# Matmul with a rotary epilogue: block pairs loaded in half rows, one tile on each half of the partitions, with mirrored weights

## The chip, the cores and the metric

The kernel runs on one core of one Trainium2 chip. The metric is the device time of one launch in microseconds (us). The engines named below are TensorE (PE, with its weight loads shown apart as PEld), VectorE (DVE), ScalarE (ACT), GpSimd (POOL) and SyncE (SP, which only issues transfers and waits). SBUF is the memory on the chip with 128 partitions, PSUM the memory that TensorE writes to.

## The reference

A batch of 16 sequences of 512 rows and 768 columns is multiplied by a 768 x 768 weight matrix; each of the 12 heads of 64 columns is then rotated with given cosines and sines. All is float32; the kernel multiplies in float16.

```python
y = np.matmul(x, weight).reshape(16, 512, 12, 64)
y1, y2 = y[..., :32], y[..., 32:]
out1 = y1 * cos[..., :32] - y2 * sin[..., :32]
out2 = y2 * cos[..., 32:] + y1 * sin[..., 32:]
```

## The kernel before

**Tiles and groups.** The 8192 rows are cut into 64 tiles of 128 rows (i = 0 to 63). Four tiles make a group g = i // 4, two tiles a pair (g, h). A group's output of 4 x 768 columns fills six PSUM banks (`py`); pair h = 0 owns banks 0 to 2, pair h = 1 banks 3 to 5. The contraction over 768 is cut into six chunks (t, e) of 128.

**Two ways to bring the contraction onto the partitions.** TensorE needs x with the contraction index on the partitions.
- A plain tile is loaded whole by one transfer from SP (`load`, L201: 128 partitions x 3072 bytes into `xs`), cast to float16 by ACT (`cast`, L236, into `xc`), transposed on TensorE (`turn`, L244, or `turn_rows`, L256, which does it with 12 small matmuls on the two row halves of the array), and copied back from PSUM by ACT (into `xt`).
- A block pair (`BLOCKS`, L137: the second pair of groups 5 to 14, ten pairs) skips TensorE's transposes. It is loaded in four quarters (`load_quarter`, L209): quarter q puts columns 192 q to 192 q + 191 of both tiles on partitions 32 q to 32 q + 31, in runs of 768 bytes. Pairs of odd groups are loaded by SP as float32 into `xb` and cast by ACT (`cast_pair`, L274, into `xd`); pairs of even groups are loaded by POOL with the cast inside the transfer (into `xh`). Then one 32 x 32 block transpose on VectorE (`turn_pair`, L282) makes `xp`, in which the contraction lies on all 128 partitions for both tiles.

**Weights.** `load_w` (L225) loads each chunk's 128 rows with one transfer from SP into `w_raw`, VectorE casts it (`cast_w`) into `w_sb`. Loads at the start are issued by SP in the order of L459: tiles 0, 1, w0, tile 2, w1, w2, tile 3, w3, w4, w5, then the tables of cosines and sines, then tile 4 and on.

**The order of the work.** Group 0 is written out by hand (L528 to L635): each weight chunk is used by the tiles as it comes (`mm0`). From tile 4 to tile 59 the array is split in two row halves of 64 rows that work side by side on different banks: `walk` (L341) lists the matmuls of a pair for row half r, `one` (L355) issues one, and `both` (L372) takes always the half that is behind in columns (half 1 starts 1024 columns later, `LAG`). Each half contributes its 64 rows of every chunk, so every bank is written by both halves; the half that closes a bank waits until the other has closed its part (`after`). When banks are complete `rope` (L393) is issued: a multiply on VectorE (L411, PSUM times cos and sin into `tq` or the space of `w_raw`), then an add on POOL (L428) into `ov`, which is stored by ACT or SP.

**Queues.** Each engine takes its instructions in the order of issue. SP issues x loads in the order of the list `fetch` (L471 to L482), held back by the buffers: ten `xs`, three `xb`. `casts`, `turns` and `bturns` place ACT's and VectorE's work 6, 4 and 4 tiles ahead of the matmuls; POOL's quarters are issued 20 tiles ahead (`pool_loads`). Stores of most groups are delayed by a group or so (L603).

Of the kernel before, what the change touches and what calls it, by code (L numbers as in the profile page):

```python
# [10 lines left out]
FP32 = mybir.dt.float32  # L11
FP16 = mybir.dt.float16
# [93 lines left out]
def kernel(  # L106
# [11 lines left out]
    f = Flow(nc, tc)  # L118
    do = f.do
    P = nc.NUM_PARTITIONS  # L120

    B, S, H = x.shape
# [3 lines left out]
    R = 32  # L126
    NQ = P // R
    NT = H // (2 * P)
    SB = S // P
    QB = 4  # L130
    NG = B * SB // QB
    NTILE = QB * NG
    CHUNKS = [(t, e) for t in range(NT) for e in range(2)]
# [1 line left out]


    BLOCKS = {}  # L137
    for g in range(5, 15):
        BLOCKS[g, 1] = "pool" if g % 2 == 0 and g >= 4 else "sp"

    def sbuf(name, shape, dt):
        return nc.alloc_sbuf_tensor(name, shape, dt).ap()

    NX, NB, NBH, NC, NCP, NXT, NXP, NOV = 10, 3, 3, 5, 2, 8, 4, 4

    ident = sbuf("ident", [P, P], FP16)
    cold = sbuf("cold", [P, 512], FP16)
# [1 line left out]
    csn = sbuf("csn", [P, 2, SB, D], FP32)  # L149
    w_raw = sbuf("w_raw", [P, NT, 2, H], FP32)  # L150
    w_sb = sbuf("w_sb", [P, NT, 2, H], FP16)
    xs_b = [sbuf(f"xs{i}", [P, H], FP32) for i in range(NX)]
    xb_b = [sbuf(f"xb{i}", [P, 2 * H], FP32) for i in range(NB)]
    xh_b = [sbuf(f"xh{i}", [P, 2 * H], FP16) for i in range(NBH)]
    xc_b = [sbuf(f"xc{i}", [P, H], FP16) for i in range(NC)]
    xd_b = [sbuf(f"xd{i}", [P, 2 * H], FP16) for i in range(NCP)]
    xt_b = [sbuf(f"xt{i}", [P, NT, 2, P], FP16) for i in range(NXT)]
    xp_b = [sbuf(f"xp{i}", [P, 2 * H], FP16) for i in range(NXP)]
    tq_mem = sbuf("tq", [P, 6144], FP32)
    w_flat = w_raw.rearrange("p t e n -> p (t e n)")  # L160
    W_HOME = [f"wr{t}{h}" for t, h in CHUNKS]

    def products(at, n, lo, hi):

# [13 lines left out]
    def ring(name, n, state={}):  # L178
        k = state.get((id(f), name), 0)
        state[id(f), name] = k + 1  # L180
        return k % n

    def copy(e, o, i_):
        return lambda eng: (
            eng.copy(out=o, in_=i_) if e == "act" else eng.tensor_copy(out=o, in_=i_)  # L185
        )

    def where(i):
        g, s = divmod(i, QB)
        return QB * (g // SB) + s, g % SB  # L190

    def pair_of(i):
        return i // QB, (i % QB) // 2

    def is_block(i):
        return pair_of(i) in BLOCKS
# [10 lines left out]
            writes=[f"xs{k}"], dma=f"xs{k}")  # L207

    def load_quarter(gh, q):  # L209
        g, h = gh  # L210
        b, r = where(g * QB + 2 * h)
        e = BLOCKS[gh]
        src = x[b : b + 2].rearrange("b (j a r) (q k) -> r q a (b j) k", r=SB, a=R, q=NQ)
        if q == 0:
            xs[gh] = ring("xh", NBH) if e == "pool" else ring("xb", NB)
        k = xs[gh]
        name = f"xh{k}" if e == "pool" else f"xb{k}"
        buf = xh_b[k] if e == "pool" else xb_b[k]
        dst = buf.rearrange("p (j k) -> p j k", j=2 * NQ)
        do(e, lambda eng: eng.dma_start(out=dst[ts(q, R)], in_=src[r, q]),  # L220
           writes=[f"{name}q{q}"], dma=name)

    wv = weight.rearrange("(p t e) n -> t e p n", t=NT, e=2)

    def load_w(c, e="sp"):  # L225
        t, h = c
        do(e, lambda eng: eng.dma_start(out=w_raw[:, t, h], in_=wv[t, h]),  # L227
           writes=[f"wr{t}{h}"], dma=f"w{t}{h}")

    def cast_w(c, e):  # L230
        t, h = c
        do(e, copy(e, w_sb[:, t, h], w_raw[:, t, h]),
           reads=[f"wr{t}{h}"], writes=[f"w{t}{h}"])


    def cast(i, e):  # L236
        k = xs[i]
        c = ring("xc", NC)
        xc[i] = c
        do(e, copy(e, xc_b[c].rearrange("p (t m e) -> p t m e", t=NT, e=2),  # L240
                   xs_b[k].rearrange("p (m t e) -> p t m e", t=NT, e=2)),
           reads=[f"xs{k}"], writes=[f"xc{c}"])

    def turn(i, e):  # L244
# [29 lines left out]
    def cast_pair(gh, e="act"):  # L274
        k = xs[gh]
        c = ring("xd", NCP)
        xc[gh] = c
        do(e, copy(e, xd_b[c].rearrange("p (t j e) -> p t j e", t=NT, e=2),
                   xb_b[k].rearrange("p (j t e) -> p t j e", t=NT, e=2)),
           reads=[f"xb{k}q{q}" for q in range(NQ)], writes=[f"xd{c}"])  # L280

    def turn_pair(gh):  # L282
        g, h = gh
        z = ring("xp", NXP)
        dst = xp_b[z].bitcast(FP32)
        if BLOCKS[gh] == "pool":
            k = xs[gh]
            src = xh_b[k].bitcast(FP32).rearrange("p (j t) -> p t j", t=NT)
            rd = [f"xh{k}q{q}" for q in range(NQ)]
        else:  # L290
            c = xc[gh]
            src, rd = xd_b[c].bitcast(FP32), [f"xd{c}"]
        v = xp_b[z].rearrange("p (t m e) -> p t e m", t=NT, e=2)
        do("dve", lambda eng: eng.transpose(out=dst, in_=src), reads=rd, writes=[f"xp{z}"])  # L294
        for s in (0, 1):
            xT[g * QB + 2 * h + s] = (
                lambda t, e, s=s: v[:, t, e, ts(s, P)], f"xp{z}")

    def units(g):
        if g < LAST:
# [37 lines left out]

    def walk(pair, r):  # L341

        g, h = divmod(pair, 2)
        for bank in ((0, 1, 2) if r == 0 else (2, 0, 1)):
            opens = (r == 0) == (bank < 2)
            lo = h * 1536 + bank * 512
            parts = [(lo, lo + 512)] if bank != 1 else [(lo, lo + 256), (lo + 256, lo + 512)]
            for a, z in parts:
                i = g * QB + a // H
                for c in CHUNKS:  # L350
                    yield z - a, (g, i, a, z, r, c, opens,
                                  opens and (a, c) == (lo, CHUNKS[0]),
                                  c == CHUNKS[-1], z == lo + 512)

    def one(g, i, a, z, r, c, opens, start, ends, whole):  # L355
        s, rows, (t, h), bank = i % QB, ts(r, HP), c, a // 512
        get, key = xT[i]
        after = closed[g, bank] if not opens and c == CHUNKS[0] else 0
        do("pe", lambda eng: eng.matmul(  # L359
            py[:, a:z], get(t, h)[rows], w_sb[rows, t, h, a - s * H : z - s * H],  # L360
            start=start, stop=not opens and ends and whole, skip_group_check=True),
            reads=[key, f"w{t}{h}"], writes=[f"ps{bank}"], tick=ends, after=after)
        if ends and whole and opens:
            closed[g, bank] = f.count["pe"]
        if ends and whole and not opens:
            ready.setdefault(g, set()).add(bank)

    ready, roped = {}, set()
# [100 lines left out]


    fetch, quarters = [], []  # L471
    soon = [p for p in sorted(BLOCKS) if BLOCKS[p] == "sp"]
    for i in range(QB, NTILE):
        if soon and i >= max(2, soon[0][0] - 1) * QB:
            quarters += [(soon[0], q) for q in (0, 2, 1, 3)]
            soon.pop(0)
        if not is_block(i):
            fetch.append(i)
            if quarters:
                fetch.append(quarters.pop(0))  # L480
        elif quarters and quarters[0][0] == pair_of(i):
            fetch.append(quarters.pop(0))  # L482
# [4 lines left out]
    def pump():  # L487

        while fetched[0] < len(fetch):
            j = fetch[fetched[0]]  # L490
            if isinstance(j, int):
                if xs_sent[0] - xs_used[0] >= NX:
                    return
                load(j)
                xs_sent[0] += 1
            else:
                if j[1] == 0:
                    if xb_sent[0] - xb_used[0] >= NB:
                        return
                    xb_sent[0] += 1  # L500
                load_quarter(*j)
            fetched[0] += 1
# [56 lines left out]
    pump()  # L559

    rows_on = [False]
    state = {"cast": 4, "turn": 4, "bturn": 0, "pool": 0}
    pairs = sorted(BLOCKS)
    pool_pairs = [p for p in pairs if BLOCKS[p] == "pool"]

    def casts(upto, most=NTILE):
        while state["cast"] < min(upto, NTILE) and most > 0:
            most -= 1
            i = state["cast"]
            state["cast"] += 1  # L570
            if not is_block(i):
                castx(i, "act")
            elif i % 2 == 0 and BLOCKS[pair_of(i)] == "sp":
                cast_pair(pair_of(i))
                xb_used[0] += 1
            pump()
# [14 lines left out]
            turn_pair(gh)  # L591
            state["bturn"] += 1

    def pool_loads(upto):
        while state["pool"] < len(pool_pairs):
            gh = pool_pairs[state["pool"]]
            if gh[0] * QB + 2 * gh[1] >= upto:
                return
            for q in (0, 2, 1, 3):
                load_quarter(gh, q)  # L600
            state["pool"] += 1

    stores = {}  # L603
    for g in range(LAST):
        for h in (0, 2):
# [9 lines left out]
                q = q[:3] + ("sp",)  # L615
            stores.setdefault(i, []).append(q)

    C_AHEAD, T_AHEAD, B_AHEAD, P_AHEAD = 5, 3, 4, 20

    for i in (0, 1):  # L620
        mm0(i, CHUNKS[5])
# [15 lines left out]
    for i in range(QB, NTILE):  # L637
# [22 lines left out]
        bturns(i + B_AHEAD)  # L660
        turns(i + 1 + (T_AHEAD if i > QB else 2), 1)
        casts(i + 1 + (C_AHEAD if i > QB else 4), 1 + i % 2)
        pool_loads(i + P_AHEAD)
        for q in stores.get(i, ()):
            store(*q)
        if g == LAST:
# [47 lines left out]
```

## Time and profile before

| what | value |
|---|---|
| median of 3 runs | 152.18 us (151.9 to 154.3) |
| the profiled execution | 152.72 us, of which the span of its instructions is 150.9 us |
| PE busy | 140.2 us (93%) |
| DVE / POOL / ACT busy | 126.8 / 122.0 / 78.3 us |
| DMA moved | 51.27 MB, mean 340 GB/s |
| loads issued by SP / by POOL, stores by ACT | 27.92 MB with the SP stores / 1.97 MB as written (float16) / 21.10 MB |

The span runs from the first instruction to the last; some 1.8 us of the execution lie around it. Busy shares are means over stages with different limits, so a stage has to be read by itself: what ended the last wait there. Durations of transfers from issue to landing include the time that they stand in the queue.

### The profile page before, as it was taken

What the parts mean: (1) busy time and instruction counts of PE and PEld (TensorE: products, weight loads), DVE (VectorE), ACT (ScalarE), POOL (GpSimd) and SP (SyncE); (2) the same over time, 40 slices, a digit from 0 to 9 for tenths busy, and PEclk for the clock granted to TensorE, in tenths of its full rate; (3) what the DMA queues carried; (4) which work ended last, traced back from release to release, by engine and by line L of the source; (5) the groups of instructions that cost most, each with busy time, mean ns of one, the idle gap of its engine ahead of it and who ended that gap; (6) DMA issues with size and microseconds to landing.
All of it is one profiled execution on the core that took longest, in us unless ns stands there. A gap on an engine that the chain in (4) does not pass through costs nothing.

```text
span 150.9 us, 4381 instructions
## 1 busy us (share of the span) xinstructions
PE 140.2 (93%) x1938; PEld 101.2 (67%) x1938; DVE 126.8 (84%) x93; ACT 78.3 (52%) x92; POOL 122.0 (81%) x67
## 2 busy tenths in 40 slices
PE   6659999999999999999999999999999999999930
PEld 2325557778777777777777777777777777776620
DVE  0244997887888899899999998999989998999990
ACT  3444688977787842548243826283436826164000
POOL 1000387799989997999999999999995979999970
PEclk9999999999999999999999999999999999999995
DMA  4999999999999999999999999999999999976574
GB/s 125 340 382 403 402 399 398 243 402 326 306 365 340 290 351 358 322 383 344 339 350 384 376 324 356 363 387 329 351 364 404 417 394 401 385 278 240 221 297 151
DMA packets 27555, 51.27 MB, mean 340 GB/s; under 512 B 7184, under 2 KB 13072, under 8 KB 27536
## 3 DMA queue, kind: packets, MB, share of 16 engines
q1 hardware_dynamic: 14592, 27.92, 53.9%
q10 hardware_dynamic: 7504, 21.10, 35.6%
q0 software_dynamic: 5440, 1.97, 10.5%
q8 instruction: 15, 0.25, 0.6%
q14 instruction: 4, 0.03, 0.1%
HBM read 27.79 MB, written 25.17 MB: 351 GB/s over the span
## 4 chain that ended last, share of the span: by engine, by line
PE 86%; DMA 5%; DVE 4%; SPq 1%; issue 1%; ACT 1%; DVEq 0%
PE py L359 72%; PE py L334 8%; DMA w_raw<-in_weight_dram 5%; PE pt L266 4%; PE pt L251 1%; DVE tq L411 1%; DVE ov L428 1%; DVE xs L411 1%; SPq L205 1%; SPq L227 1%; ACT xt L185 1%; DVE w_sb L185 0%; SPq L709 0%; DVEq L57 0%; SPq L116 0%
## 5 line engine op out<-in xcount | busy, mean ns | idle before, releaser
L428 POOL TENSOR_TENSOR ov<-tq 128x1536 f32<-128x1536 f32 (+3 forms) x29 | 75.4, 2620 | 19.9 <-DVE tq L411 19.8
L359 PE MATMUL py<-w_sb,xt 64*128 64x256 f16 (+1 forms) x864 | 80.7, 323 | 0.0
L411 DVE TENSOR_TENSOR tq<-py,csn 128x1024 f32<-128x1024 f32 (+2 forms) x45 | 74.1, 1676 | 5.4 <-PE py L359 5.0
L359 PEld LDWEIGHTS py<-w_sb,xt 64*128 64x128 f16 x864 | 53.3, 94 | 17.6 <-DVE tq L411 0.4
L185 ACT COPY xt<-pt 128x768 f16<-128x768 f16 x42 | 33.5, 800 | 42.1 <-PE pt L266 38.0
L185 ACT CAST xc<-xs 128x768 f16<-128x768 f32 x44 | 39.2, 905 | 18.2 <-DMA xs<-in_x_dram 17.9
L359 PE MATMUL py<-w_sb,xp 64*128 64x256 f16 (+1 forms) x480 | 46.8, 323 | 0.0
L411 DVE TENSOR_TENSOR w_raw<-py,csn 128x1024 f32<-128x1024 f32 (+1 forms) x21 | 35.2, 1676 | 4.4 <-PE py L359 4.2
L428 POOL TENSOR_TENSOR ov<-w_raw 128x1536 f32<-128x1536 f32 (+1 forms) x12 | 35.0, 2921 | 3.7 <-DVE w_raw L411 3.4
L359 PEld LDWEIGHTS py<-w_sb,xp 64*128 64x128 f16 x480 | 30.4, 94 | 9.5
L334 PE MATMUL py<-w_sb,xt 128*128 128x256 f16 (+1 forms) x90 | 15.7, 323 | 1.9 <-DVE w_sb L185 1.6
L266 PEld LDWEIGHTS pt<-ident,xc 64*128 64x128 f16 x432 | 14.1, 95 | 1.8 <-ACT xt L185 0.6
L334 PEld LDWEIGHTS py<-w_sb,xt 128*128 128x128 f16 x90 | 8.1, 98 | 7.7 <-DVE w_sb L185 3.2
L266 PE MATMUL pt<-ident,xc 64*128 64x64 f16 x432 | 12.4, 190 | 0.3 <-ACT xt L185 0.3
L220 POOL DMA_DIRECT2D xh<-in_x_dram x20 | 11.6, 589 | 0.0
L185 ACT CAST xd<-xb 128x1536 f16<-128x1536 f32 x5 | 8.2, 1638 | 0.1
L185 DVE CAST w_sb<-w_raw 128x768 f16<-128x768 f32 x6 | 3.4, 560 | 4.4 <-DMA w_raw<-in_weight_dram 4.4
L294 DVE STREAM_TRANSPOSE xp<-xh 128x768 f32<-128x768 f32 x5 | 6.2, 1237 | 0.0
L510 PE MATMUL py<-cold 128*128 128x512 f16 x12 | 4.2, 512 | 1.4 <-DVE cold L453 1.4
L185 DVE COPY xt<-pt 128x768 f16<-128x768 f16 x2 | 1.1, 558 | 4.9 <-PE pt L251 4.9
L251 PE MATMUL pt<-ident,xc 128*128 128x128 f16 x48 | 4.0, 220 | 0.9 <-ACT xc L185 0.9
L251 PEld LDWEIGHTS pt<-ident,xc 128*128 128x128 f16 x48 | 2.9, 98 | 3.0 <-ACT xc L185 2.0
(17 smaller groups left out, 15.4 us busy)
## 6 DMA issues: line engine op xcount, KB each, us to landing
out_dram<-ov ACTq DMA_DIRECT2D x26, 768.0 KB, 9.1
xs<-in_x_dram SPq DMA_DIRECT2D x44, 384.0 KB, 16.8
xb<-in_x_dram SPq DMA_DIRECT2D x20, 192.0 KB, 16.1
out_dram<-ov SPq DMA_DIRECT2D x4, 768.0 KB, 3.9
w_raw<-in_weight_dram SPq DMA_DIRECT2D x6, 384.0 KB, 7.7
xh<-in_x_dram POOLq DMA_DIRECT2D x20, 96.0 KB, 13.2
out_dram<-ov SPq DMA_DIRECT2D x1, 384.0 KB, 2.3
out_dram<-ov ACTq DMA_DIRECT2D x1, 384.0 KB, 2.3
```

The source lines that it names most:

```text
L185: eng.copy(out=o, in_=i_) if e == "act" else eng.tensor_copy(out=o, in_=i_)
L205: do(e, lambda eng: eng.dma_start(out=xs_b[k], in_=x[b].rearrange("(p r) h -> r p h", r=SB)[r]), writes=[f"xs{k}"], dma=f"xs{k}")
L220: do(e, lambda eng: eng.dma_start(out=dst[ts(q, R)], in_=src[r, q]), writes=[f"{name}q{q}"], dma=name)
L227: do(e, lambda eng: eng.dma_start(out=w_raw[:, t, h], in_=wv[t, h]), writes=[f"wr{t}{h}"], dma=f"w{t}{h}")
L251: do("pe", lambda eng: eng.transpose(pt[:, t, h, :], src[:, t, h, :], ident), reads=[f"xc{c}", "ident"], writes=[f"pt{k}"], tick=(t, h) == ...
L266: do("pe", lambda eng: eng.transpose(pts[r][:, t, h, :], src[rows, t, h, :], ident[rows, rows]), reads=[f"xc{c}", "ident"], writes=[f"pt{r ...
L294: do("dve", lambda eng: eng.transpose(out=dst, in_=src), reads=rd, writes=[f"xp{z}"])
L334: do("pe", lambda eng: eng.matmul(ps, get(t, h), w_sb[:, t, h, a - s * H : z - s * H], start=start, stop=stop), reads=[key, f"w{t}{h}"], w ...
L359: do("pe", lambda eng: eng.matmul(py[:, a:z], get(t, h)[rows], w_sb[rows, t, h, a - s * H : z - s * H], start=start, stop=not opens and en ...
L411: do("dve", lambda eng: eng.tensor_tensor(out=tq.rearrange("p j (h d) -> p j h d", d=D), in0=ps.rearrange("p (h d) -> p h d", d=D) .unsque ...
L428: do(adder, lambda eng: eng.tensor_tensor(out=ov_b[o][:, ds(c0, w)].rearrange("p (h t d) -> p h t d", t=2, d=HD), in0=tq[:, 0].rearrange(" ...
L510: do("pe", lambda eng: eng.matmul(py[:, ts(b, 512)], cold[:, 0:P], cold, start=True, stop=warmed[0] < WARM - 6), reads=["cold"], writes=[f ...
```

## The change

Twelve pairs (the second pair of groups 3 to 14) are block pairs, and SP loads all of them as float32; POOL issues no transfer, and `xh`, its cast inside the transfer and `pool_loads` are gone. `xb` has four buffers. A quarter now holds half rows of one tile: quarters 0 and 1 put the two halves of the rows of the first tile on partitions 0 to 63, quarters 2 and 3 those of the second tile on partitions 64 to 127, in runs of 1536 bytes. After VectorE's transpose, a tile's whole contraction lies on its own 64 partitions in 12 chunks of 64, and row half r of the array does tile r alone. For that each half of the partitions needs all weight rows: `w_sb` holds one half, and `w_un` gets the other by two transfers inside SBUF (`mirror`), issued by SP at tile 14's place in `fetch`. The rows of the weights are numbered so that plain tiles use the same `w_sb`; each chunk of the weights is loaded by two transfers of 64 partitions instead of one of 128. In `walk` a block pair's bank 0 and bank 2 are written by one row half only, bank 1 by both. Quarters stand in `fetch` at their own pair's place.

```diff
-    for g in range(5, 15):
-        BLOCKS[g, 1] = "pool" if g % 2 == 0 and g >= 4 else "sp"
+    for g in range(3, 15):
+        BLOCKS[g, 1] = "sp"
-    NX, NB, NBH, NC, NCP, NXT, NXP, NOV = 10, 3, 3, 5, 2, 8, 4, 4
+    NX, NB, NC, NCP, NXT, NXP, NOV = 10, 4, 5, 2, 8, 4, 4
+    w_un = sbuf("w_un", [P, NT, 2, H], FP16)
...
-        src = x[b : b + 2].rearrange("b (j a r) (q k) -> r q a (b j) k", r=SB, a=R, q=NQ)
+        b, r = where(g * QB + 2 * h + q // 2)
+        src = x[b].rearrange("(j a r) (q k) -> r q a j k", r=SB, a=R, q=2)[r, q % 2]
...
-    wv = weight.rearrange("(p t e) n -> t e p n", t=NT, e=2)
+    wv = weight.rearrange("(m u t e) n -> t e u m n", u=2, t=NT, e=2)
...
-        do(e, lambda eng: eng.dma_start(out=w_raw[:, t, h], in_=wv[t, h]),
-           writes=[f"wr{t}{h}"], dma=f"w{t}{h}")
+        for u in range(2):
+            do(e, lambda eng: eng.dma_start(out=w_raw[ts(u, HP), t, h], in_=wv[t, h, u]),
+               writes=[f"wr{t}{h}{u}"], dma=f"w{t}{h}")
...
-        do(e, copy(e, xc_b[c].rearrange("p (t m e) -> p t m e", t=NT, e=2),
-                   xs_b[k].rearrange("p (m t e) -> p t m e", t=NT, e=2)),
+        do(e, copy(e, xc_b[c].rearrange("p (t u m e) -> p t u m e", t=NT, u=2, e=2),
+                   xs_b[k].rearrange("p (m u t e) -> p t u m e", t=NT, u=2, e=2)),
...
+    def mirror():
+        for u in range(2):
+            do("sp", lambda eng: eng.dma_start(
+                out=w_un[ts(1 - u, HP)].rearrange("p t e n -> p (t e n)"),
+                in_=w_sb[ts(u, HP)].rearrange("p t e n -> p (t e n)")),
+                reads=[f"w{t}{h}" for t, h in CHUNKS], writes=[f"v{u}"], dma=f"v{u}")
...
+        if gh in BLOCKS:
+            plan = ([("only", [(0, 512)]), ("close", [(512, 768)])] if r == 0 else
+                    [("open", [(768, 1024)]), ("only", [(1024, 1536)])])
...
+                    for t in range(2 * NT):
+                        own = (t < NT) == (r == 0)
+                        u, tt = t // NT, t % NT
+                        for c in range(2):
+                            w = (w_sb if own else w_un)[rows, tt, c, n0 : n0 + cols]
...
-        if soon and i >= max(2, soon[0][0] - 1) * QB:
+        if soon and i >= soon[0][0] * QB + 2 * soon[0][1] - 4:
...
+        if i == soon_mirror:
+            fetch.append("mirror")
```

## The prediction

> **What bounds the kernel now.** I read the page's first two parts and its chain, then the timelines of VectorE, PE and ACT over the start, then the table by windows.
>
> ```profile
> span 150.9 us, 4381 instructions
> PE 140.2 (93%) x1938; PEld 101.2 (67%) x1938; DVE 126.8 (84%) x93; ACT 78.3 (52%) x92; POOL 122.0 (81%) x67
> ...
> PE   6659999999999999999999999999999999999930
> ...
> PE 86%; DMA 5%; DVE 4%; SPq 1%; issue 1%; ACT 1%; DVEq 0%
> ```
>
> PE is dense from the fourth slice to the last two, and the chain of work lies on it for 86%. So only two kinds of edit show in the time: what changes PE's own work, and what delays it. The 5% that the chain spends on DMA is the wait for the weights at the start. VectorE's timeline shows when they land, since it casts each at once:
>
> ```profile
> 9.71 0.56 DVE L185 CAST w_sb<-w_raw 128x768 f16<-128x768 f32 x1 [1.38 <-DMA w_raw<-in_weight_dram]
> 10.65 0.56 DVE L185 CAST w_sb<-w_raw 128x768 f16<-128x768 f32 x1 [0.38 <-DMA w_raw<-in_weight_dram]
> 12.62 0.56 DVE L185 CAST w_sb<-w_raw 128x768 f16<-128x768 f32 x1 [1.40 <-DMA w_raw<-in_weight_dram]
> 13.59 0.56 DVE L185 CAST w_sb<-w_raw 128x768 f16<-128x768 f32 x1 [0.42 <-DMA w_raw<-in_weight_dram]
> 14.59 0.56 DVE L185 CAST w_sb<-w_raw 128x768 f16<-128x768 f32 x1 [0.43 <-DMA w_raw<-in_weight_dram]
> ```
>
> Neighbours in the queue land 0.97 us apart (10.65 and 9.71; 13.59 and 12.62): 0.393 MB in 0.97 us is 405 GB/s, and the queue is never empty, for the third weight is issued at 3.27 us and lands at 10.63. Behind the weights stand the tables and tile 4, which lands at 16.28; ACT casts it at once, and PE's chain takes it at once:
>
> ```profile
> 12.74 0.33 PE pt L251 x6
> 13.08 4.25 PE py L334 x26
> 17.33 0.43 PE pt L251 x6
> 17.76 0.65 PE py L334 x4
> 18.41 0.35 PE pt L251 x6
> 18.76 0.33 PE py L334 x2
> 19.09 2.17 PE py L359 x16
> ```
>
> (start, length, what). The transpose at 17.33 is tile 4's, whose cast ends at about 17.25; the one at 18.41 is tile 5's, landed at 17.25. Group 0's banks, too, come free for PE only after products that need the last weight. So PE has no slack here: whatever delays the sixth weight and tile 4 delays PE's dense run, and the end, one for one.
>
> How fast transfers go depends on their shape and their company:
>
> ```profile
> 14.00:20.00 6.00, 6.00 (x46) 3.09 (x45) 5.24 (x7) 3.62 (x5) 1.85 (x2) 1.00 1.04 402
> 27.00:30.00 3.00, 3.00 (x50) 2.15 (x47) 2.34 (x3) 2.64 (x4) 2.74 (x1) 1.00 1.05 232
> 30.00:34.00 4.00, 4.00 (x73) 3.04 (x71) 3.27 (x3) 2.95 (x5) 3.98 (x6) 1.00 1.03 397
> 100.68:108.83 8.15, 8.15 (x134) 6.19 (x126) 8.00 (x6) 3.67 (x5) 7.88 (x3) 1.00 1.14 343
> 35.00:43.50 8.50, 8.50 (x147) 6.54 (x145) 7.03 (x5) 6.40 (x8) 8.47 (x3) 1.00 1.15 318
> ```
>
> (window, length, busy time of PE, PEld, DVE, ACT, POOL, clock, DMA share, GB/s.) Loads over all 128 partitions alone: 402. The same queue with quarters of 32 partitions among the tiles and no stores yet: 232, with the engines as busy; a tile's packet of 3072 bytes then takes about 226 ns instead of 121 to 125. With stores beside them: 397.
>
> **The change part by part.** The sum is made against the profiled execution, 152.72 us (150.9 us of span, 1.8 around it), which is 0.54 above the median of 152.18.
>
> *PE's transposes.* Two plain pairs (groups 3 and 4) become block pairs: four turns of 0.18 us (the chain's steps of L266, 12 matmuls each) go, -0.72. The windows agree: a group without a block pair takes 8.50 us, with one 8.15; two groups, -0.70. The matmuls stay: 2 x 9216 columns per pair, 24 per row half before (6 chunks x 4 pieces) and after (12 chunks x 2 pieces), and the halves still use different banks. Waits of one half for the other fall from three a pair to one; the chain shows none that costs, so nothing is gained.
>
> *VectorE.* 12 block transposes of 0.97 us (the form from `xd`) in place of 5 of 0.97 and 5 of 1.24: +0.6. It is busy 8.00 of 8.15 us in a group with such a pair, so it still fits; were the new layout to cost 1.24 it would need 8.27 a group, as the groups with a POOL pair do now without holding PE. Taken 0, bound 1.4 (12 x 0.12).
>
> *ACT.* Seven more casts of 1.63, four casts of 0.905 and four copies of 0.80 fewer: +4.6 us, under 3.67 of 8.15 us busy per group. The casts read pairs of numbers 48 bytes apart instead of 24, which no row shows; both casts cost 0.95 ns per further element ((1638 - 905) / 768), so I take the same. 0.
>
> *POOL.* 20 issues of 0.589 us (11.6 us) go. It waits for products, not PE for it: 0.
>
> *Transfers in the middle.* The cast transfers of POOL go, 5120 packets of 49 ns, and 5120 of SP's at 47; 6144 packets of 1536 bytes come, between 65 ns (on the line from 36 at 768 bytes to 121 at 3072) and 113 (half the 226). Four plain tiles go (512 packets of 130). In engine time over 16 engines: -30.7 - 4.2 + (25 to 43) = -10 to +8 us, in stages with stores nearer the first, since quarters took 36 ns beside stores once POOL's were done. `mirror` adds 1.18 MB: 2.9 us of queue at 405 GB/s, 5.1 at 232. Cover: tile 16 lands 7.0 us before its cast, tile 17 5.7, tile 20 none but 2.2 us before its transpose; and two pairs (1.57 MB, 4 us) that were loaded ahead of tile 20 now stand behind it. The copies must also land before tile 14's matmuls at about 41 us; tile 13 lands at 26, then quarters (2 to 3.4 us) and copies (2.9 to 5.1): 37 at the latest. Taken 0, bounds 0 and +1.5 (tile 20: 2.2 + 4 - 5.1 - 2.9 at worst). SP's 28 more quarter issues cost 0.43 each, 12 us, on a queue that stands blocked by full rings for most of 27 to 108 us: 0.
>
> *The weights at the start.* Six transfers of 128 partitions become twelve of 64. Six more issues of 0.43 us do not show: SP is 7 us ahead. The transfers are the same packets of 3072 bytes, so they cannot be faster than 405 GB/s: lower end 0. No row has a 64-partition load; the nearest is the stretch of 27 to 30 us, part-partition loads among tiles with no stores, as at the start: 232 GB/s, 1.69 us a weight instead of 0.97, 6 x 0.72 = +4.3. If tiles 2 and 3 among them slow down as the tiles did there, 8 x 0.72 = +5.8, the upper end. I take +4.3, since nothing else in the trace is as near: no stores, one queue, parts of the partitions. It goes to the end in full (above).
>
> [...]
>
> Sum: -0.7 + 4.3 = +3.6; 152.72 + 3.6 = 156.3 for a profiled run, 155.8 against the median.
>
> **The rivals.**
> - *The halves overlap at the start* (the other side: not slower). The 16 engines do not stay in step: one tile's shares landed between 14.89 and 16.28 us. If an engine that is ahead works on the second half while its neighbour is on the first, both halves of the memory are written at once and a weight still takes 0.97 us. For it: the first quarters at 26 us still ran at 36 ns a packet, full speed. Against it: a microsecond later everything fell to half, and stayed so until stores came. Then 152.18 - 0.7 = 151.5. In between (a third of the loss, 1.4) 152.9. It decides at a delay of 0.7 us: below that the time is no longer than before.
> - *The middle runs dry.* Copies and quarters fall into a stretch without stores and ACT's casts wait, so PE's transposes do: the start's +4.3 and 1.5 to 3 more, 157.3 to 158.8. For it: tiles 33, 37, 41, 45, 49 and 53 are cast in the very moment they land, so the loads are the scarce thing there, and tile 53's transpose begins only 2.3 us after its cast. Against it: the engine time above falls beside stores, and quarters no longer run a group ahead of the tiles.
> - *Part of the delay is swallowed.* For it: PE has 0.9 us of idle time at 21.6, where it waits for ACT. Against it: ACT's work there follows the same loads. 155.8 - 0.9 = 154.9.
>
> **How the numbers follow.** A difference of about 2%, 3.0 us, is what a measurement of this kernel can tell from no change: 155.2 is the bound. The likeliest case, weights at about half rate: 50%, 154.9 to 157.5, a tenth of it under the bound. Halves that overlap: 25%, 151.3 to 152.6. In between, swallowed in part or half overlapped: 13%, 152.6 to 154.9. The middle runs dry as well: 12%, 157.3 to 158.8 and a little over; 0.10 of it above the bound, 0.01 after a fast start, and 0.01 I keep for a gain. Slower: 0.45 + 0.10 = 0.55. Within 2%: 0.05 + 0.25 + 0.13 + 0.01 = 0.44. Faster by over 2%: 0.01; PE alone would have to lose 3 us of work, and the change takes 0.7. The range leaves out a tenth or less at each end: 151.5 to 158.5.
>
> **What would show it.** Right: VectorE's casts of the weights 1.5 to 1.9 us apart where they were 0.97, the last at 18 to 20 us instead of 14.59; PE's first L359 at 22.5 to 24 instead of 19.09; GB/s of the second to fourth slice well under 340 to 400; a group of 8.15 us from group 3 on and no PE gap between. Wrong: weight casts still 0.97 us apart (the first rival), or waits of PE for ACT or for the copies between 35 and 60 us (the second); a transpose of 1.24 or a slower cast would show in the groups' rows.

## The result and the profile after

The changed kernel takes 163.52 us in the median of 4 runs (162.22 to 165.09); the kernel before took 152.7 beside it (4 runs). The ratio is 1.0699, 95% interval 1.0587 to 1.0810: slower by 10.8 us, where 3.6 were forecast. The profiled execution of after is its longest, 165.09 us with a span of 163.3. In this section and the next a ratio leaves disturbed runs out, so it is not always the quotient of the two medians, and the profiles of after, of the halves on two queues, of the middle partitions and of twelve pairs by SyncE are of such runs. The median of the kernel before, taken anew beside each set of runs, was 151.8 to 152.7 us, so a difference between runs of different sets is good to about 1 us.

The page of after, its parts on busy time, slices and the chain:

```profile
span 163.3 us, 4302 instructions
PE 145.5 (89%) x1890; PEld 110.9 (68%) x1890; DVE 128.3 (79%) x95; ACT 82.0 (50%) x91; POOL 110.9 (68%) x47
...
PE   6759899898986898999999989889999999999950
...
GB/s 153 287 257 239 324 404 249 269 237 321 402 363 218 306 408 258 371 409 358 387 359 360 386 381 365 332 400 323 412 364 408 334 417 387 414 394 328 265 313 169
...
DMA 32%; PE 29%; SPq 26%; ACT 4%; DVE 3%; issue 3%; DVEq 0%
```

PE's slices have holes from the fifth on, and the chain, which lay on PE for 86%, now lies on transfers and on SyncE's queue for 58%. The GB/s row moves between about 240 and 400, slice by slice. Two places explain the time. First the start, in VectorE's timeline of after (weight casts) and then PE's:

```profile
10.37 0.56 DVE L185 CAST w_sb<-w_raw 128x768 f16<-128x768 f32 x1 [2.12 <-DMA w_raw<-in_weight_dram]
12.00 0.56 DVE L185 CAST w_sb<-w_raw 128x768 f16<-128x768 f32 x1 [1.07 <-DMA w_raw<-in_weight_dram]
14.98 0.56 DVE L185 CAST w_sb<-w_raw 128x768 f16<-128x768 f32 x1 [2.42 <-DMA w_raw<-in_weight_dram]
16.62 0.56 DVE L185 CAST w_sb<-w_raw 128x768 f16<-128x768 f32 x1 [1.08 <-DMA w_raw<-in_weight_dram]
18.26 0.56 DVE L185 CAST w_sb<-w_raw 128x768 f16<-128x768 f32 x1 [1.07 <-DMA w_raw<-in_weight_dram]
```

```profile
22.58 2.39 PE L376 MATMUL py<-w_sb,xt 64*128 64x512 f16 x19
...
50.24 0.35 PE L264 MATMUL pt<-ident,xc 64*128 64x64 f16 x12 [1.82 <-ACT xt L185]
...
53.97 3.51 PE L376 MATMUL py<-w_sb,xt 64*128 64x512 f16 x40 [0.78 <-ACT xt L185]
```

Neighbouring weights land 1.63 us apart instead of 0.97, the last cast is at 18.26 instead of 14.59, and the dense run begins at 22.58 instead of 19.04: 3.54 us. The last two lines belong to the second place, the middle: PE waits for ACT's copies. ACT's waits in after, from the list of waits (total, times, longest), and the first of them in before, against which they stand:

```profile
ACT xc L185 <- DMA xs<-in_x_dram: 34.3, 18, 4.0
ACT xd L185 <- DMA xb<-in_x_dram: 15.9, 10, 2.4
```

```profile
ACT xc L185 <- DMA xs<-in_x_dram: 17.9, 9, 3.1
```

Before, nine tiles were waited for and no pair; after, 18 tiles and 10 of 12 pairs. ACT's timeline of after shows how such a wait reaches PE:

```profile
45.17 0.88 ACT L185 CAST xc<-xs 128x768 f16<-128x768 f32 x1 [3.98 <-DMA xs<-in_x_dram]
48.62 0.87 ACT L185 CAST xc<-xs 128x768 f16<-128x768 f32 x1 [2.57 <-DMA xs<-in_x_dram]
48.62 0.39 ACTq L465 DMA_DIRECT2D out_dram<-ov  x1
49.40 0.79 ACT L185 COPY xt<-pt 128x768 f16<-128x768 f16 x1
51.55 1.57 ACT L185 CAST xd<-xb 128x1536 f16<-128x1536 f32 x1 [1.37 <-DMA xb<-in_x_dram]
53.03 0.79 ACT L185 COPY xt<-pt 128x768 f16<-128x768 f16 x1
```

The cast at 48.62 waits 2.57 us for a tile; the copy behind it ends at 50.19, and PE's transpose starts at 50.24. The cast at 51.55 holds the copy at 53.03, and PE starts at 53.97. ACT's store, too, is issued only at 48.62, behind the cast: while ACT waits for loads no new store starts. What that does to the loads is in the windows of after (columns as before):

```profile
23.00:33.00 10.00, 9.21 (x154) 6.39 (x154) 7.66 (x5) 7.84 (x11) 8.12 (x4) 1.00 1.07 277
33.00:40.00 7.00, 6.33 (x103) 5.64 (x98) 6.08 (x4) 5.53 (x6) 4.73 (x2) 1.00 1.00 271
40.00:47.00 7.00, 6.92 (x102) 5.57 (x103) 5.53 (x6) 1.68 (x2) 4.55 (x2) 1.00 1.04 400
49.00:55.00 6.00, 3.98 (x53) 2.55 (x55) 3.29 (x4) 4.23 (x5) 3.77 (x2) 1.00 1.08 220
23.00:148.00 125.00, 118.30 (x1725) 95.97 (x1723) 108.74 (x69) 71.00 (x79) 98.16 (x32) 1.00 1.04 354
```

and of before over its own dense run:

```profile
23.00:33.00 10.00, 10.00 (x177) 7.68 (x173) 8.12 (x5) 8.12 (x12) 8.11 (x7) 1.00 1.05 340
23.00:140.00 117.00, 117.00 (x1758) 88.43 (x1753) 107.73 (x69) 65.69 (x78) 110.08 (x54) 1.00 1.06 351
```

The DMA share, last column but one, is above 1 in both: on the mean the engines that move data had a packet under way all the time before, too. (It is a sum of packet times over 16 engines, so at 1.06 and 1.04 some packets of one engine overlapped.) The copies were issued at 20.54 and 21.08 us and landed at 40.46 and 43.16; tile 16, which before landed at 30.86, lands at 45.15 and is cast in that moment (the first line of ACT's timeline); in the run without the copies, below, it lands at 36.05. From there on the loads only keep pace.

The account in the two profiled executions, by the start of the last run of products (138.62 before, 151.34 after, +12.7): 3.5 at the start, -0.7 for four turns saved, and 9.9 between, of which 8.0 lie in eleven stalls of PE of 0.1 to 2.0 us, between 31 and 132 us (counted from start to start of its matmuls, less the usual 0.2; a short wait at 26.05 is in before too, at 22.49). The other 1.9 was not traced. Nine of the eleven follow a copy of ACT. Two, at 31.41 and 40.08 (0.7 each), show no releaser, but the transfers offer one: packets of 16384 bytes on the queue that the profile calls "instruction" landed at 29.81 and 38.45, and PE goes on 1.60 and 1.63 us later. In the run with whole weights, below, such packets landed at 25.69 and 34.65, and PE goes on after a stall without releaser at 27.22 and 36.16, 1.53 and 1.51 us later. So these two look like PE waiting for its own instructions, brought through the same crowded transfers; no run tested it. The profiled run being 1.6 us above its median, the middle costs some 8 us in the median: 10.8 - 3.5 + 0.7.

### The profile page after: what moved, and what is told of

The parts are those of the page before. It is cut to its first block, busy times and chain, and to the rows that moved or that the text cites. A ratio compares the mean times of both kernels' runs of the same rounds, so it can differ in the third digit from the quotient of the medians.

```text
span 163.3 us, 4302 instructions
## 1 busy us (share of the span) xinstructions
PE 145.5 (89%) x1890; PEld 110.9 (68%) x1890; DVE 128.3 (79%) x95; ACT 82.0 (50%) x91; POOL 110.9 (68%) x47
## 4 chain that ended last, share of the span: by engine, by line
DMA 32%; PE 29%; SPq 26%; ACT 4%; DVE 3%; issue 3%; DVEq 0%
DMA xb<-in_x_dram 26%; PE py L376 24%; SPq L217 15%; SPq L205 6%; DMA xs<-in_x_dram 5%; SPq L225 4%; PE py L331 3%; ACT xt L185 2%; ACT xc L185 2%; PE pt L264 1%; ACT xd L185 1%; DVE tq L427 1%; DVE xs L427 1%; DVE ov L444 1%; PE pt L249 1%
## 5 line engine op out<-in xcount | busy, mean ns | idle before, releaser
L376 PE MATMUL py<-w_sb,xt 64*128 64x256 f16 (+1 forms) x768 | 76.9, 323 | 3.9 <-ACT xt L185 3.1
L185 ACT CAST xc<-xs 128x768 f16<-128x768 f32 x40 | 35.0, 883 | 34.4 <-DMA xs<-in_x_dram 34.3
L376 PE MATMUL py<-w_sb,xp 64*128 64x512 f16 (+1 forms) x288 | 47.8, 323 | 0.0
L376 PE MATMUL py<-w_un,xp 64*128 64x256 f16 (+1 forms) x288 | 44.6, 323 | 0.0
L185 ACT COPY xt<-pt 128x768 f16<-128x768 f16 x38 | 30.2, 797 | 19.2 <-PE pt L264 14.1
L185 ACT CAST xd<-xb 128x1536 f16<-128x1536 f32 x12 | 19.0, 1584 | 15.9 <-DMA xb<-in_x_dram 15.9
L376 PEld LDWEIGHTS py<-w_sb,xp 64*128 64x128 f16 x288 | 25.4, 94 | 2.0
L376 PEld LDWEIGHTS py<-w_un,xp 64*128 64x128 f16 x288 | 24.9, 94 | 2.1
L264 PE MATMUL pt<-ident,xc 64*128 64x64 f16 x384 | 14.8, 191 | 2.8 <-ACT xt L185 2.1
L287 DVE STREAM_TRANSPOSE xp<-xd 128x768 f32<-128x768 f32 x12 | 11.7, 973 | 2.4 <-ACT xd L185 2.4
```

Of the source, the lines that this page charges most:

```text
L264: do("pe", lambda eng: eng.transpose(pts[r][:, t, h, :], src[rows, t, h, :], ident[rows, rows]), reads=[f"xc{c}", "ident"], writes=[f"pt{r ...
L376: do("pe", lambda eng: eng.matmul(ps, x_, w_, start=start, stop=mode != "open" and last, skip_group_check=True), reads=keys, writes=[f"ps{ ...
```

## The experiments

The theory: a transfer that writes only partitions 0 to 63 or 64 to 127 runs at about half the rate unless stores run beside it (from 8 to 12 us after moved 244 GB/s and before 393; from 49 to 55 after moved 220). At the start this costs what was forecast; in the middle the narrow quarters and the copies do the same, and no engine time was left to pay for it. The rivals: it is the number of transfers or the packet's size; one queue is the limit; the extra pairs, or the move of all quarters to SyncE, cost the time whatever the layout.

### The start alone, and the three narrow things one by one

**Halves in the kernel before.**

```diff
-        do(e, lambda eng: eng.dma_start(out=w_raw[:, t, h], in_=wv[t, h]),
+        for u in range(2):
+            do(e, lambda eng: eng.dma_start(out=w_raw[ts(u, HP), t, h], in_=wv[t, h, ts(u, HP)]),
```

> The kernel before, with each weight chunk loaded by two transfers of 64 partitions instead of one of 128; nothing else. If the halves cost what they seem to in the changed kernel (its first L376 is 3.54 us later than the first L359 before), the last weight lands near 18.2 us instead of 14.56 and the time is 152.7 + 3.5 = 156.2. If that delay comes from something else of the change (the new order of rows, the casts with the wider step), 152.7.

155.82 us, ratio 1.0254 (1.0222 to 1.0287), +4.0. In its trace the last weight cast is at 17.74 and the dense run starts at 22.12, 3.1 later than before; no stall follows that before does not have, and its profiled execution is 3.1 us longer. So the start's term stands by itself, and it goes to the end one for one.

**No copies.**

```diff
-                            w = (w_sb if own else w_un)[rows, tt, c, n0 : n0 + cols]
+                            w = w_sb[rows, tt, c, n0 : n0 + cols]
...
-            fetch.append("mirror")
+            pass
```

> The changed kernel without the two copies inside SBUF: both row halves read w_sb, so half of the block pairs' weights are the wrong rows. If the copies alone starve the loads in the middle, all PE stalls after 30 us go with them (8 us): 155.5. If the narrow quarters are the cause and the copies only add to it, the stalls near 50 and 54 us go (2.9 us) and the 0.2 to 1.2 us per group from 60 us on stay: 160 to 161.

157.44 us, 1.0388 (1.0320 to 1.0456): 6.1 less than after. The time is between the two expectations, but the stalls went as in the first: after 40 us one of 0.2 us is left, and from the dense run's start to the last run of products 119.8 us pass, where before has 119.6 and after 128.8. What the profiled execution (157.01) has over 155.5 is the start: its dense run begins only at 23.71. The granted clock of TensorE was 0.50 from 12 to 16 us there, 0.63 in after and 1.00 in before.

**Whole weights** (the transfer of before, other rows).

> The changed kernel with each weight chunk loaded by one transfer of 128 partitions, in the order of rows of the kernel before, so the weights used are other rows. If the halves are the start's whole loss: 163.5 - 3.5 = 160.0 and the first L376 at 19.0 us. If the middle takes the gain back (the loads there come no earlier): 162 to 163.5.

160.76 us, 1.0581 (1.0527 to 1.0634): 2.8 less than after, while 7.5 us of stalls stay. The middle's cost does not hang on the start's.

**Wide quarters.**

```diff
-        src = x[b].rearrange("(j a r) (q k) -> r q a j k", r=SB, a=R, q=2)[r, q % 2]
+        src = x[b].rearrange("(p r) (q k) -> r q p k", r=SB, q=2)[r, q % 2]
...
-        do(e, lambda eng: eng.dma_start(out=dst[ts(q, R)], in_=src),
+        do(e, lambda eng: eng.dma_start(out=dst[:, q], in_=src),
```

> The changed kernel with each quarter's 128 packets of 1536 bytes spread over all 128 partitions instead of 32; the block pairs' data lie in the wrong places. If transfers to few partitions are what runs at half rate without stores, the stretches at 49 to 55 and 62 to 65 us go from 210 to 220 GB/s to near 400, the per-group stalls vanish and so do most of those near 50: 163.5 - 7 = 156.5. If the size of the packets, one queue for all loads or the order of the loads is the cause, 162 to 163.5.

156.60 us, 1.0292 (1.0245 to 1.0338): 6.9 less than after, by the same 6144 packets of 1536 bytes. The windows of this run:

```profile
49.00:55.00 6.00, 5.64 (x80) 4.21 (x77) 5.06 (x5) 3.67 (x6) 4.93 (x2) 1.00 1.04 410
62.00:65.00 3.00, 3.00 (x60) 2.75 (x55) 2.79 (x2) 2.74 (x3) 2.77 (x1) 1.00 1.03 409
23.00:148.00 125.00, 123.88 (x1787) 104.91 (x1786) 115.94 (x76) 71.03 (x81) 106.64 (x38) 1.00 0.98 371
```

410 where after has 220. The mean times of packets after 23 us, from the trace's packet records, put side by side (ns; "beside stores" when a store's packet ended in the same microsecond):

| run | quarters of 1536 bytes, beside stores / alone | tiles of 3072 bytes, beside stores / alone |
|---|---|---|
| after | 75 / 112 | 139 / 189 |
| no copies | 74 / 97 | 138 / 159 |
| wide quarters | 65 / 68 | 124 / 128 |

The narrow quarters slow the whole tiles down with them, and only wide ones cost the same with and without stores. No copies or wide quarters: each alone takes back 5 to 7 us, which is most of the 8. So neither the narrow quarters nor the copies are enough by themselves. From the dense run's start to the last run of products, with twelve pairs, 118.9 us pass with neither (the next run), 119.8 with the narrow quarters alone, 120.3 with the copies alone and 128.8 with both: about 1 us each, and 10 together.

**All three undone.** The three edits above together.

> The changed kernel with whole weight loads, quarters over 128 partitions and no copies together (the block pairs' data and weights are then others). If these three are the whole loss, what is left is the saved transposes: 151.8 - 0.7 = 151.1, first L376 at 19.0, no PE wait for ACT after 23 us. If the new walk, the casts with the wider step or the order of the quarters cost something of their own, 152.5 or more.

150.91 us, 0.9923 (0.9896 to 0.9950). The dense run starts at 18.60, and after 23 us PE waits for nothing:

```profile
23.00:33.00 10.00, 10.00 (x177) 7.67 (x173) 8.27 (x6) 8.03 (x11) 7.43 (x3) 1.00 1.03 396
23.00:140.00 117.00, 117.00 (x1710) 89.51 (x1705) 110.26 (x72) 66.97 (x76) 100.27 (x34) 1.00 0.94 366
```

The account closes: what remains, 1.2, is the 0.7 of saved turns and a dense run that begins 0.4 earlier in the trace. The DMA share is 0.94, so the loads have slack here that neither kernel has. It doesn't compute the reference, so it is a bound and not a version.

### Is it the half of the partitions?

**Column halves, middle partitions.** The kernel before, with each weight in two transfers: once in column halves over all 128 partitions, once as 64 partitions each, but partitions 32 to 95.

```diff
+            cols = ts(u, H // 2)
+            do(e, lambda eng: eng.dma_start(out=w_raw[:, t, h, cols], in_=wv[t, h][:, cols]),
```

```diff
+        mid, n = ds(R, 2 * R), 2 * t + h
+        for u, to in enumerate((w_raw[:, t, h], spare)):
+            do(e, lambda eng: eng.dma_start(out=to[mid], in_=wv[t, h, ts(u, HP)]),
```

> The kernel before with each weight chunk loaded by two transfers again, but cut by columns: 128 partitions x 1536 bytes each. If the cost of the halves (4.0 us measured) is that they go to few partitions, this costs nothing: 151.8 to 152.2, weight casts 0.97 us apart. If it is the number of transfers or their smaller packets, 154 to 156.

> The kernel before with each weight chunk's bytes loaded by two transfers of 64 partitions, both to partitions 32 to 95 (the second into spare memory; the outer partitions are zeros, so a third of the weights are other numbers). [...] If 64 partitions are slow wherever they lie: as the halves, 155.8, last cast near 18 us.

Column halves: 152.52 us, 1.0016 (0.9978 to 1.0053); twice the transfers and half the packet cost nothing. Middle partitions: 153.72 us, 1.0086 (1.0041 to 1.0131), the last cast at 14.19 and the dense run from 19.58, nearly as before. The window of 8 to 12 us in the run with partitions 32 to 95:

```profile
8.00:12.00 4.00, 3.53 (x24) 1.81 (x25) 1.32 (x4) 2.30 (x3) 0.00 (x0) 1.00 1.02 381
```

and in the halves of the kernel before, then in after:

```profile
8.00:12.00 4.00, 2.16 (x14) 0.96 (x14) 1.00 (x3) 1.68 (x2) 0.00 (x0) 1.00 1.03 275
8.00:12.00 4.00, 2.16 (x14) 0.96 (x14) 0.81 (x2) 1.66 (x2) 0.00 (x0) 1.00 1.02 244
```

The same number of partitions, bytes and transfers: 381 against 275 and 244 GB/s. So it isn't the number of partitions, but which ones. What sets 32 to 95 apart from 0 to 63 and 64 to 127 was not shown.

**Two queues.** In the changed kernel, the upper halves of the weights issued by ACT, or the second tile's quarters.

```diff
+            do(("sp", "act")[u], lambda eng: eng.dma_start(out=w_raw[ts(u, HP), t, h], in_=wv[t, h, u]),
```

> The changed kernel with the lower half of each weight chunk issued by SP and the upper half by ACT, so that both halves are in flight at once from two queues. If a 64-partition load is slow because all engines write one half of the partitions at a time, both halves are now written together: the last weight lands near 15 us, the start's loss of about 4 us mostly goes, the first L376 at 19 to 20 us, and the time is 160 to 161 as with whole weights. If two loads to the two halves get in each other's way whichever queue they come from, it stays at 163.5.

> The changed kernel with the quarters of each pair's second tile (upper partitions) issued by ACT instead of SP. If narrow transfers are slow only while nothing writes the other partitions, loads from two queues fill both: the stretches without stores rise above 300 GB/s and most of the 8 us of stalls go: 156 to 158. If the narrow quarters are slow whatever runs beside them, or now stand behind ACT's stores, 162 to 166.

166.25 us, 1.0835 (1.0754 to 1.0916), the dense run not before 25.44; and 165.44 us, 1.0866 (1.0801 to 1.0931), still with some 10 us of stalls. With both halves in flight on two queues, 8 to 14 us moved 281 GB/s, where the halves on one queue in the kernel before moved 265 and its whole weights 396. So two queues did not write both halves at once at the full rate. The times of these two runs show less: in the first the granted clock was 0.50 to 0.64 from 8 to 20 us, which holds the dense run back as well (the last weight is cast at 19.95, 1.7 later than in after, the dense run begins 2.9 later), and in the second the quarters now stand behind ACT's stores, as its expectation allowed for.

### The pairs and their queue

**Twelve pairs in the kernel before**, its own quarters (POOL's with the cast inside).

```diff
-    for g in range(5, 15):
+    for g in range(3, 15):
```

> The kernel before with twelve block pairs instead of ten (groups 3 and 4 too, odd groups by SP, even ones by POOL), its own quarters and nothing else of the change. If the two pairs are worth their four turns and their loads hide: 151.8 - 0.7 = 151.1. If the narrow quarters come too early, before any store, and PE waits: 152 to 154.

155.37 us (152.78 to 158.41, 10 runs), 1.0101 (1.0055 to 1.0148), with short waits of PE for ACT at 84.55 and 120.76. The extra pairs alone do not pay. Why this one spreads so widely stays open.

**Ten pairs with late copies, and with whole weights.** The changed kernel with groups 5 to 14, so that the copies go at tile 22; then also with weights loaded whole, which splits each quarter into two transfers with runs of 768 bytes.

> The changed kernel with ten block pairs (groups 5 to 14 as before the change), so that quarters and copies come where stores already run; weights in halves still. If the middle's loss comes from copies and narrow quarters meeting in the stretch without stores, PE's waits for ACT go: 151.8 + 4.0 = 155.8 to 156.5. If the loads of every group are too slow in any case, 159 to 162.

> As the run with ten pairs and late copies, but with the contraction numbered so that each weight chunk is again one transfer of 128 partitions; each quarter is then two transfers with runs of 768 bytes. PE's work is that of the kernel before. If start and middle are both mended: 151.8 to 152.5, the first L376 at 19.0. If the copies or the smaller runs still hold the loads back: 154 to 158.

159.46 us, 1.0481 (1.0385 to 1.0577), and 160.81 us, 1.0567 (1.0477 to 1.0656). In the second the start is mended (18.53), yet PE stalls at 73.5 us (2.58) and from 109 to 127. Its expectation was missed by 8 us. So something of the middle was neither the number of pairs nor the early place of the copies. Four more runs looked for it: the kernel before with all ten pairs by SyncE; that, with quarters placed as the change places them; that, with twelve pairs; and the 160.81 version without copies.

```diff
-        BLOCKS[g, 1] = "pool" if g % 2 == 0 and g >= 4 else "sp"
+        BLOCKS[g, 1] = "sp"
...
-        if soon and i >= max(2, soon[0][0] - 1) * QB:
+        if soon and i >= soon[0][0] * QB + 2 * soon[0][1] - 4:
```

> The kernel before, with its ten pairs, whole weights and quarters of 768-byte runs, but all quarters loaded by SyncE as float32 (four xb buffers); nothing else. It tests the second part of the change's description alone. If narrow quarters on one queue are enough to run the loads dry (the residue of the two runs with ten pairs), ACT waits for loads in the late groups and PE for ACT: 155 to 159 us. If they are not, because the quarters stay covered by stores, the time is that of the kernel before with at most 1 us more, 152 to 153.5.

> The run before this one with the quarters placed in the queue as the change places them, at their own pair's place instead of a group ahead among the tiles. If the place matters (four quarters in a row behind each other, in front of the next tiles), PE waits for ACT that the first of the two does not show, and it is 1 us or more slower than that one. If not, both agree within 0.7 us.

> As the run before this one with twelve pairs, groups 3 to 14: everything of the change but half rows, weights in halves and copies. If the copies and the weights are what the rest of the loss hangs on, it stays near the kernel with the copies left out less the start's 4 us, 153 to 154. If twelve narrow pairs alone keep the loads short, 156 or more.

> The version with ten pairs and weights loaded whole (160.8 us), with the two copies left out, so that both row halves use the same half of the weights in block pairs and the rows of those pairs are not the reference's. If the copies alone took the lead that is missing at 73 us and later, 152 to 153.5. If quarters as eight transfers with 768-byte runs at their own pair's place are the cause, 156 to 160 remains.

| run | median us | ratio (interval) |
|---|---|---|
| all ten pairs by SyncE | 156.15 | 1.0262 (1.0216 to 1.0307) |
| and quarters placed late | 155.58 | 1.0234 (1.0195 to 1.0274) |
| and twelve pairs | 160.78 | 1.0444 (1.0373 to 1.0515) |
| half rows, whole weights, no copies, ten pairs | 155.69 | 1.0226 (1.0169 to 1.0282) |

The part of the change that looked free, moving POOL's quarters to SyncE, costs 4 us by itself in the kernel before, where quarters have runs of 768 bytes. PE's timeline of that first run has the loss late, in 3.1 us of stalls:

```profile
112.09 3.51 PE L359 MATMUL py<-w_sb,xt 64*128 64x512 f16 x40 [1.30 <-ACT xt L185]
...
121.87 3.51 PE L359 MATMUL py<-w_sb,xt 64*128 64x512 f16 x40 [1.36 <-ACT xt L185]
...
130.72 3.51 PE L359 MATMUL py<-w_sb,xt 64*128 64x512 f16 x40 [0.43 <-ACT xt L185]
```

and the window of its last third shows the shortfall (the other two thirds have PE at 37.00 of 37 and 40.00 of 40):

```profile
100.00:135.00 35.00, 31.90 (x458) 25.25 (x452) 29.75 (x21) 18.33 (x20) 28.04 (x10) 1.00 1.04 361
```

Where the quarters stand in the queue makes no difference (155.58 and 156.15). Two more pairs cost 3 us by the ratios and 5 by the medians. Half rows in 768-byte runs cost nothing (155.69 and 155.58), and the copies cost 5.1 (160.81 and 155.69). The long runs of 1536 bytes are a gain: the run without copies, less the start's 4.0, is at 153.4 with twelve pairs, and the one with 768-byte runs at 160.78. With ten pairs and the copies it is the same: 159.46 less 4.0, against 160.81. A quarter's 1536 bytes take 77 ns in the run without copies, and 94 in two packets of 47. So in the changed layout the move to SyncE did not cost 4 us: the run with all three undone has it with twelve pairs and loses nothing, the run without copies has it and loses about 1.

## Why the prediction was wrong, step by step

- **PE's transposes, -0.7:** right (38 copies of `xt` by ACT instead of 42; four turns gone).
- **VectorE, ACT and POOL, 0:** right. The transposes from `xd` take 973 ns in the new layout, the casts of pairs 1584 ns and of tiles 883, less than the 1638 and 905 before. ACT's 82.0 us busy never were the limit; what held PE was ACT's waiting.
- **The weights at the start, +4.3:** right in mechanism and nearly in size: +3.5 in the trace; in the run that has this part alone +3.1 in the trace and +4.0 in the median. A weight took 1.63 us where 1.69 was worked out from the window of 232 GB/s (which was not quite free of stores: 36 of its 402 packets). The first rival, halves that overlap, is out: the weights landed 1.63 us apart, and two queues moved 281 GB/s from 8 to 14 us, where the whole weights of before moved 396.
- **Transfers in the middle, "Taken 0, bounds 0 and +1.5":** this step failed. It cost some 8 us. In engine time (all packets that end after the dense run's start, over 16 engines) before has 134.9 us and after 141.1, +6.2: the quarters 31.0 for the 30.7 of POOL's and SyncE's old ones (25 to 43 forecast), the copies 4.2, the stores 1.7 more, and the whole tiles the same 37.9 though four of them went (4.2), because their packets grew from 136 to 151 ns. The sum lies inside the -10 to +8 of the forecast. What failed is what I set this against. I used the leads of tiles 16, 17 and 20, 2 to 7 us, as cover for a burst. But the DMA share of 1.06 over the whole dense run, in before, leaves little engine time that could refill a lead once it is spent. The copies were priced at 2.9 to 5.1 us of queue; tile 16, behind them, landed at 45.15 with them and at 36.05 without, 9.1 us. They landed at 43.16 where I had 37 at the latest. (The terms given there add up to 34.5 at most, and those of the worst case for tile 20 to -1.8, not 1.5.) After that the narrow stretches without stores were paid by PE: the copies alone or the narrow quarters alone were covered but for about 1 us, and together they were not. Side by side, each from one execution:

| run | engine time from the dense run's start, us | from there to the last run of products, us |
|---|---|---|
| all three undone | 121.3 | 118.9 |
| wide quarters | 127.0 | 120.3 |
| no copies | 132.1 | 119.8 |
| ten pairs, late copies | 133.8 | 123.4 |
| second tile's quarters by ACT | 134.4 | 129.6 |
| before | 134.9 | 119.6 |
| half rows, ten pairs, no copies; all ten pairs by SyncE | 136.2; 136.2 | 123.6; 123.6 |
| twelve pairs in the kernel before | 138.7 | 121.6 |
| after; ten pairs, whole weights | 141.1; 141.1 | 128.8; 127.7 |
| twelve pairs by SyncE | 144.5 | 130.4 |

More engine time goes with a longer run on the whole, but it does not decide: ten pairs with late copies and the second tile's quarters by ACT lose 4 and 11 us below the 134.9 of before, and twelve pairs in the kernel before lose only 2 or 3 above it. Where in the run and behind which queue the transfers stand counts too. And a packet's time depends on its company (a whole tile's took 189 ns among narrow quarters without stores, 128 among wide ones), so the sum is a sign as much as a cause.

- **The move of POOL's quarters to SyncE, part of the same step:** counted only as engine time. Alone, in the kernel before, it costs 4 us, with 1.3 us more of packets and the DMA share down from 1.08 to 1.05 between 23 and 135 us. My reading is that a third queue kept more packets in flight; that is argued and not shown, since no run had quarters in float32 on a queue of their own beside stores by ACT and tiles by SyncE. Two rivals stand untested: the same move raises the bytes moved from 51.27 to 53.24 MB, since half of the quarters arrived as float16 before, and it gives ACT five more casts of pairs (busy 85.4 us instead of 78.3).
- **The sign that would make it wrong** was the right one: waits of PE for ACT between 35 and 60 us, the longest of after (50.24) among them. The rival "the middle runs dry" had the mechanism, at 12% and 1.5 to 3 us. It was priced as one burst; the wait came back in most groups. As the timeline reads, that is because ACT issues stores behind casts that wait for loads, and with few or no stores beside them the loads of after ran at 220 to 277 GB/s.

Open: whether the two stalls without a releaser are waits for instructions; why copies and narrow quarters cost so much more together than apart; how much of the recurring waits is the loop through ACT's late stores, which was read from the timeline and not tried; and the third queue's part.

## What to carry to other kernels

Before a lead is counted as cover, look at the DMA share over the whole stretch: at the 1.06 of before a lead that the change spent had little to refill it, and two costs that it nearly covered one by one broke it together. Read the rate of a transfer from a stretch where no stores run beside it: narrow quarters took 75 ns beside stores and 112 without, and there 220 GB/s were moved where wide ones had 410. So undo parts together as well as one by one: here either of two cost about 1 us, and both 10. And undo "who issues it" as a part of its own: with runs of 768 bytes it cost 4 us, with wide quarters of 1536 nothing.

## What the runs showed of the hardware

- In after and in the halves of the kernel before, stretches with transfers within partitions 0 to 63 or 64 to 127 moved 220 to 277 GB/s with few or no stores beside them, and 128-partition tiles in the same queue slowed down with them (189 ns a packet in after, 128 with wide quarters). With weights on partitions 32 to 95 it was 381 from 8 to 12 us, where after moved 244.
- Beside stores the same narrow quarters took 75 ns instead of 112, at some 400 GB/s in all (40 to 47 us of after).
- Copies from one half of the partitions to the other took 525 ns for a packet of 9216 bytes in after, 347 to 948; three packets of 3072 at the 128 of a lone wide tile would be 384, an estimate from the table above. The fastest are below that estimate, so it is not the copy as such that was slow.
- Where the halves held PE up at the start, the granted clock fell in some executions: from 12 to 16 us it was 0.50 without copies and on two queues, 0.63 in after, and 1.00 in before and in the halves of the kernel before.
